# Pair 7's turned probabilities are sent from SP's queue, and the last norm's sums stand one unit later

## The chip, the core and the metric

The program runs on one core of a Trainium2 chip. That core has five engines with a queue of instructions each: TensorE (PE, matmuls; its weight loads are listed apart as PEld), VectorE (DVE), ScalarE (ACT), GpSimd (POOL) and SyncE (SP), which here only issues DMAs. Each engine takes its instructions strictly in the order of the program; they meet through semaphores. A DMA is issued by an instruction in the queue of SP, ACT or POOL and then moved by 16 DMA engines that all queues share. The metric is the device time of one execution in microseconds (us). Before the change it is 640.57 us, the median of 3 runs (640.5 to 640.58).

## What is computed

Two residual layers over 256 tokens of width 1024, float32: layer 0 mixes the tokens with forgetting attention, layer 1 with block attention plus a relative-position bias (with 256 tokens there is one block, so it is causal attention). Behind each mixer come a SwiGLU feed-forward part and a gated embedding, and one norm ends it.

```
for i in range(DEPTH):
    u = _rmsnorm(h, attn_norm_g[i])
    ...
        o = _fox_attention(q, k, v, log_f)
        h = h + _merge_heads(o) @ fox_w_o[j]
    ...
    u = _rmsnorm(h, ffn_norm_g[i])
    gu = u @ ffn_w_in[i]
    h = h + (jax.nn.silu(gu[..., :D_FF]) * gu[..., D_FF:]) @ ffn_w_out[i]
    gate = jax.nn.sigmoid(_rmsnorm(h, ple_norm_g[i]) @ ple_w_gate[i])
    h = h + gate * (p[i] @ ple_w_up[i])
return _rmsnorm(h, final_norm_g)
```

## The kernel before

**Weights.** The float32 weights are streamed in chunks of 128x1024 in the order of use. SP loads a chunk into one of six buffers (`raw`, lines 138, 154 and 186; line 186 loads chunks with a gap in them, 128x1080). ScalarE rounds it to a first half (`whi`, lines 139, 169, 187) and VectorE subtracts to get the rest (`wlo`, lines 142, 171, 188). A product is then three matmuls (lines 94, 95, 96): high by high, high by low, low by high. SP may load into a `raw` buffer again when VectorE has made `wlo` from it, and `whi` and `wlo` have six buffers each, free when TensorE has used them.

**The end of an attention.** The 16 heads go in 8 pairs, 0 to 7. For each pair TensorE makes the scores, VectorE adds the bias or mask (L606), ScalarE makes the exponentials (L610) and scales them (L629). `turn` (lines 632 to 661) then transposes the probabilities on VectorE in blocks of 32 (tile `turn`, L644) and moves the blocks between partitions by DMA into the tile `pt`, from which `values` (lines 667 to 681) multiplies them with `v` into the bank `po` (L674, L676); the result is split into the tile `o` (L319 on ScalarE, L320 on VectorE). Pairs 0 to 4 go through DRAM, pairs 5 to 7 straight from SBUF in four DMAs of 96 KB each (L651). Which queue issues those four is the line

```
queue = nc.scalar if j == NP - 1 else nc.gpsimd
```

so pair 6's stand on POOL and pair 7's on ScalarE. The output projection `wo` has 8 parts (`PARTS`), each with one weight chunk. The order of the end is written out by hand: parts 0, 1 and 2, then `values(4)` (pairs 4 and 5), parts 3 and 4, `values(6)` (pairs 6 and 7), parts 5 and 6, and part 7. ScalarE has, in the same stretch, the scaling of pairs 6 and 7 (L629), two copies into `v` (L513), pair 7's four DMAs (L651) and then the rounding of the weights of part 3 (L139) and of what follows. In layer 0 the chunks of parts 3 and 4 are called whi_1324 and whi_1355, and those of the feed-forward part begin with raw_1519 and raw_1525.

**The last gate.** In layer 1, `ple` (lines 865 to 990) multiplies by the gate's weights in units (`pair_unit`) of two blocks of 128 input channels: four units c = 0 to 3 of 12 matmuls (128x512) for the first half of the output (tile `pg`), then the second half. The norm's factor is applied behind them, by token. `column_root` (lines 277 to 288) makes that factor: `total` adds up the squares on VectorE (L234, L236), two matmuls with a column of ones sum over the channels (bank `pr`, L284), VectorE scales (`ms`, L286), POOL takes the root (`col`, L288). A small activation (L108) loads ScalarE's table for the sigmoid and waits for `col`. `by_token` (lines 894 to 902) turns the residual: four transposes on VectorE (L898) and eight DMAs (L902), two of them on ScalarE's queue and six on SP's. The gates (L913) need `col` and `pg`; the additions (L916) need the turned residual. The second half ends with a narrow bank `pgl`, whose gate, addition, sum of squares (L957), root (L960), scaling (L986, L989) and output DMAs (L964) close the program.

What the scheduler makes of this is a fixed order for each engine; the matmuls L284, called behind unit 1, stood in the middle of unit 2.

Of the kernel before, what the change touches and what calls it, by code (L numbers as in the profile page):

```python
# [38 lines left out]
NP = H // 2  # L39
# [36 lines left out]
def trunk(ctx: ExitStack, tc: tile.TileContext, xg, wx, xr, pt, w, cst, gf, rel, hot, rvm, out):  # L76
    nc = tc.nc
# [28 lines left out]
    def table(func, after=None):  # L106

        nc.scalar.activation(warm, ones if after is None else after, func)  # L108
# [184 lines left out]
    nm = Norm(0)  # L293
# [33 lines left out]
    def pair_unit(bks, c, wt, x, ts=(0, 1), mid=None):  # L327

        for kk in range(2):
            k = 2 * c + kk  # L330
            if kk and mid:
                mid()
            for t in ts:
                tokens(bks[t], x(k), t, [w[:, kk * HC:(kk + 1) * HC] for w in wt], k == 0, k == KT - 1)
# [125 lines left out]
    def attention(layer, nm, mid, early, nf):  # L460
# [84 lines left out]
        def project(j, a):  # L545
# [31 lines left out]
            with tc.issue_after(got.ins):  # L577
                for back in [turn(*x[:2]) for x in far]:
                    back()
# [52 lines left out]
        def turn(j, e):  # L632

            near = j >= DIRECT
            t = work.tile([P, 4, 3, 2, 32], F32, tag="e", bufs=4, name=f"turn{layer}_{j}")  # L640
            for s in range(2):
                src = e[:, s].rearrange("p (b y c) -> p b c y", b=3, c=4) if near else \
                      e[:, s].rearrange("p (b c x) -> p b c x", b=3, x=32)
                nc.vector.transpose(t[:, :, :, s].rearrange("p c b x -> p b c x"), src)  # L644
            p = work.tile([P, 4, 3, 2, 32], F32, tag="pt", bufs=4, name=f"pt{layer}_{j}")
            for s in range(2):
                pts[2 * j + s] = p[:, :, :, s].rearrange("p c b x -> p b c x")
            if near:
                queue = nc.scalar if j == NP - 1 else nc.gpsimd
                for a in range(4):  # L650
                    queue.dma_start(p[:, a].rearrange("p b s x -> p (b s x)"),  # L651
                                    t[32 * a:32 * a + 32].rearrange("p c b s x -> p (c b s x)"))
                return lambda: None
            d = dram.tile([P, 6 * P], F32, name=f"dt{layer}_{j}")
            nc.gpsimd.dma_start(d, t.rearrange("p c b s x -> p (c b s x)"))

            def back():
                for i in range(4):
                    nc.gpsimd.dma_start(p[32 * i:32 * i + 32].rearrange("p c b s x -> p c (b s x)"),
                                        bass.AP(tensor=d.tensor, offset=d.offset + 192 * i,  # L660
                                                ap=[[6 * P, 32], [32 * 6 * P, 4], [1, 192]]))

            return back
# [71 lines left out]
        for x in fresh:  # L735
            scaled(*x)
            turn(*x[:2])
# [127 lines left out]
    def ple(layer, nm, ut, nx):  # L865
# [28 lines left out]
        def by_token(hf):  # L894

            o = end[:, hf].rearrange("p (c t m x) -> p c t m x", c=4, t=2, m=4)
            for t in range(2):
                nc.vector.transpose(o[:, :, t].rearrange("p c m x -> p m c x"),  # L898
                                    h[:, 4 * hf:4 * hf + 4, t * P:(t + 1) * P].rearrange("p m (y c) -> p m c y", c=4))
            for a in range(4):  # L900
                queue = nc.scalar if hf == 0 and a % 2 else nc.sync
                queue.dma_start(ht[:, hf, a].rearrange("p t x -> p (t x)"), end[32 * a:32 * a + 32, hf])  # L902
# [21 lines left out]
        for c in range(4):  # L924
            pair_unit(bks[0], c, half(), nm.k)
            if c == 1:
                with tc.issue_after(nm.column_root().ins):
                    nc.gpsimd.drain()
                table(AF.Sigmoid, nm.col[:, 0:1])
                with tc.issue_after(nm.added.ins):  # L930
                    for hf in range(2):
                        by_token(hf)
        for t in range(2):
            gate(bks[0][t], t, 0, HC)

# [45 lines left out]
        for c0 in (0, HC):  # L981
            c = slice(c0, c0 + HC)
# [9 lines left out]
    for layer in range(2):  # L992
        nf = Norm(3 * layer + 1)
        if layer == 0:
            attention(0, nm, fox_bias, first, nf)
        else:
            attention(1, nm, lambda _: (lambda: moba[2]), [], nf)
        got = []
        np_ = Norm(3 * layer + 2)
        ffn(layer, nf, lambda pp=None: ple_in(layer) if pp is None else got.append(ple_up(layer, pp)), np_)  # L1000
        nm = Norm(3) if layer == 0 else None
        ple(layer, np_, got[0], nm)
# [123 lines left out]
```

## Time and profile before

| what | value |
|---|---|
| median of 3 runs | 640.57 us |
| the profiled execution: its own time | 640.69 us |
| its span, first to last instruction | 638.9 us |
| what lies around the span | 1.79 us |
| TensorE busy | 627.0 us, 98% |
| VectorE, ScalarE, POOL busy | 467.1, 384.6, 42.6 us |
| mean granted TensorE clock | 0.995 |
| weight loads of SP (L154 and L138: 177; L186: 36) | 512 and 540 KB each, 4.4 and 4.5 us to landing |

Start times are us from the start of the span. A row of the timeline gives start, duration, engine, line, operation, output<-input and count; behind it in brackets the idle time of the engine ahead of it and what ended that. "ACTq" and "SPq" are the queues' own instructions, DMAs above all; POOL's DMAs are listed under POOL. A matmul's duration covers the way through the array, so two of 0.28 us can start 0.11 us apart: what counts is the distance between starts. "DMA to landing" runs from the start of the issue to the arrival of the data.

### The profile page before, as it was taken

How to read it: one execution, taken by the hardware profiler on the slowest of the kernel's cores; microseconds unless marked ns; L12 is line 12 of the kernel's file. 1: busy time of each engine (PE TensorE's matmuls, PEld its weight loads, DVE VectorE, ACT ScalarE, POOL GpSimd, SP SyncE). 2: the span in 40 equal slices, each digit the busy share in tenths (PEclk: the TensorE clock that was granted, in tenths of full speed). 3: DMA queues.
4: the chain of work that ended last, by engine and by line, in shares of the span. 5: the costliest groups of instructions: out<-in, count | busy, mean ns of one | idle time of the engine just before them, and what ended most of it. 6: DMA issues, size and time to landing. Idle time of an engine off the chain costs nothing.

```text
span 638.9 us, 13102 instructions
## 1 busy us (share of the span) xinstructions
PE 627.0 (98%) x5241; PEld 604.9 (95%) x5241; DVE 467.1 (73%) x757; ACT 384.6 (60%) x663; POOL 42.6 (7%) x85
## 2 busy tenths in 40 slices
PE   9999989999999999999999999999999999999995
PEld 7899879999999999999989998899999999999984
DVE  7888868886666666668894898788666666666695
ACT  6668866764444445448774798767544444454753
POOL 0103340000000000000000054100000000000001
PEclk9999998999999999999999999999999999999999
DMA  9768878397766566666574697865866666665522
GB/s 341 248 203 242 265 215 287 100 330 259 270 202 199 187 198 214 197 208 177 192 235 171 210 297 216 261 222 170 257 192 194 198 198 199 199 210 180 191 47 86
DMA packets 41885, 135.27 MB, mean 212 GB/s; under 512 B 5248, under 2 KB 10848, under 8 KB 41824
## 3 DMA queue, kind: packets, MB, share of 16 engines
q1 hardware_dynamic: 36464, 123.33, 60.3%
q0 software_dynamic: 3488, 9.44, 5.0%
q10 hardware_dynamic: 1872, 1.67, 0.9%
q8 instruction: 41, 0.67, 0.4%
q14 instruction: 20, 0.16, 0.1%
HBM read 126.01 MB, written 8.15 MB: 210 GB/s over the span
## 4 chain that ended last, share of the span: by engine, by line
PE 82%; DVE 8%; ACT 3%; issue 2%; DMA 2%; SPq 1%; ACTq 1%; POOL 1%; DVEq 0%; POOLq 0%
PE gu L95 13%; PE gu L94 13%; PE gu L96 13%; PE fo L96 6%; PE fo L94 6%; PE fo L95 6%; PE pq L94 3%; PE pq L96 3%; PE pq L95 3%; DVE wlo L171 2%; DVE turn L644 2%; PE v L456 2%; PE wo L94 2%; PE wo L96 2%; PE wo L95 2%
## 5 line engine op out<-in xcount | busy, mean ns | idle before, releaser
L171 DVE TENSOR_TENSOR wlo<-raw,whi 128x1024 fp32r<-128x1024 f32 (+1 forms) x168 | 203.3, 1215 | 65.2 <-ACT whi L169 65.1
L169 ACT ACTIVATE whi<-raw 128x1024 fp32r<-128x1024 f32 x166 | 173.6, 1055 | 95.1 <-issue 42.5
L95 PE MATMUL gu<-g,whi 128*128 128x256 f32 x704 | 194.9, 277 | 0.0
L94 PE MATMUL gu<-g,whi 128*128 128x256 f32 x704 | 194.8, 277 | 0.0
L96 PE MATMUL gu<-g,wlo 128*128 128x256 f32 x704 | 194.7, 277 | 0.0
L96 PEld LDWEIGHTS gu<-g,wlo 128*128 128x128 f32 x704 | 132.3, 188 | 0.0
L95 PEld LDWEIGHTS gu<-g,whi 128*128 128x128 f32 x704 | 132.2, 188 | 0.1
L94 PEld LDWEIGHTS gu<-g,whi 128*128 128x128 f32 x704 | 132.3, 188 | 0.0
L96 PE MATMUL fo<-fp,wlo 128*128 128x256 f32 x352 | 97.4, 277 | 0.0
L95 PE MATMUL fo<-fp,whi 128*128 128x256 f32 x352 | 97.3, 276 | 0.0
L94 PE MATMUL fo<-fp,whi 128*128 128x256 f32 x352 | 97.2, 276 | 0.0
L94 PE MATMUL pq<-g,whi 128*128 128x256 f32 x256 | 71.5, 279 | 0.0
L96 PE MATMUL pq<-g,wlo 128*128 128x256 f32 x256 | 70.9, 277 | 0.1
L95 PE MATMUL pq<-g,whi 128*128 128x256 f32 x256 | 70.8, 277 | 0.0
L188 DVE TENSOR_TENSOR wlo<-raw,whi 128x1080 fp32r<-128x1080 f32 x36 | 45.9, 1281 | 29.8 <-ACT whi L187 29.4
L94 PEld LDWEIGHTS fo<-fp,whi 128*128 128x128 f32 x352 | 66.1, 188 | 0.0
L95 PEld LDWEIGHTS fo<-fp,whi 128*128 128x128 f32 x352 | 66.1, 188 | 0.0
L96 PEld LDWEIGHTS fo<-fp,wlo 128*128 128x128 f32 x352 | 66.1, 188 | 0.0
L187 ACT ACTIVATE whi<-raw 128x1080 fp32r<-128x1080 f32 x36 | 39.6, 1102 | 27.9 <-PE gu L95 27.1
L94 PEld LDWEIGHTS pq<-g,whi 128*128 128x128 f32 x256 | 48.1, 188 | 1.0 <-issue 0.3
L96 PEld LDWEIGHTS pq<-g,wlo 128*128 128x128 f32 x256 | 48.1, 188 | 0.3 <-DVE wlo L171 0.3
L95 PEld LDWEIGHTS pq<-g,whi 128*128 128x128 f32 x256 | 48.1, 188 | 0.1
(194 smaller groups left out, 1043.7 us busy)
## 6 DMA issues: line engine op xcount, KB each, us to landing
raw<-w SPq DMA_DIRECT2D x177, 512.0 KB, 4.4
raw<-w SPq DMA_DIRECT2D x36, 540.0 KB, 4.5
dt<-turn POOLq DMA_DIRECT2D x10, 384.0 KB, 3.4
pt<-dt POOLq DMA_DIRECT2D x40, 96.0 KB, 5.4
d<-d SPq DMA_DIRECT2D x4, 768.0 KB, 7.0
bias<-d SPq DMA_DIRECT2D x4, 512.0 KB, 7.1
pt<-turn POOLq DMA_DIRECT2D x16, 96.0 KB, 4.0
pt<-turn ACTq DMA_DIRECT2D x8, 96.0 KB, 3.7
```

Source lines behind the costliest of these rows:

```text
L94: mm(o, ah, bh, start=start, stop=False, skip_group_check=True)
L95: mm(o, ah, bl, start=False, stop=False, skip_group_check=True)
L96: return mm(o, al, bh, start=False, stop=stop, skip_group_check=True)
L169: state["hi"] = state[f"hi{i}"] = nc.scalar.activation(hi[:, c], raw[:, c], AF.Copy)
L171: nc.vector.tensor_tensor(lo[:, c], raw[:, c], f32(hi[:, c]), op=ALU.subtract)
L187: nc.scalar.activation(ht, raw[:, 0:WW], AF.Copy)
L188: state["lo"] = nc.vector.tensor_tensor(lt, raw[:, 0:WW], f32(ht), op=ALU.subtract)
L456: got = mm(bks[2 * t + hf], x[a][:, t * P:(t + 1) * P], w[b][:, hf * HC:(hf + 1) * HC], start=k + a + b == 0, stop=k + b == KT, skip_group ...
L644: nc.vector.transpose(t[:, :, :, s].rearrange("p c b x -> p b c x"), src)
```

## The change

Two edits. Pair 7's four DMAs in `turn` are issued by SP instead of ScalarE, in both layers. In the last gate `total` and `by_token` stay behind unit 1, while `column_root` (two matmuls, the scaling and POOL's root), POOL's drain and the small activation that loads the table go behind unit 2.

```
@@ -646,7 +646,7 @@
             if near:
-                queue = nc.scalar if j == NP - 1 else nc.gpsimd
+                queue = nc.sync if j == NP - 1 else nc.gpsimd
                 for a in range(4):
                     queue.dma_start(p[:, a].rearrange("p b s x -> p (b s x)"),
                                     t[32 * a:32 * a + 32].rearrange("p c b s x -> p (c b s x)"))
@@ -924,12 +924,14 @@
         for c in range(4):
             pair_unit(bks[0], c, half(), nm.k)
             if c == 1:
+                nm.total()
+                with tc.issue_after(nm.added.ins):
+                    for hf in range(2):
+                        by_token(hf)
+            if c == 2:
                 with tc.issue_after(nm.column_root().ins):
                     nc.gpsimd.drain()
                 table(AF.Sigmoid, nm.col[:, 0:1])
-                with tc.issue_after(nm.added.ins):
-                    for hf in range(2):
-                        by_token(hf)
```

At the end of layer 0's attention, ScalarE's queue loses the four DMAs that stood between the copies into `v` and the rounding of part 3's weights (whi_1324):

```order
 L513 ACTIVATE v<-v_1_165,col_302 128x512
 L513 ACTIVATE v<-v_3_167,col_302 128x512
-L651 DMA pt_7_1217<-turn_7_1214 128x1x192 x4
 L139 ACTIVATE whi_1324<-raw_1323 128x1024
 L169 ACTIVATE whi_1355<-raw_1354 128x1024
```

In the same place SP's queue gets them between the first two weight loads of the feed-forward part:

```order
 L154 DMA raw_1471<-w 128x1024
 L186 DMA raw_1519<-w 128x1080
+L651 DMA pt_7_1217<-turn_7_1214 128x1x192 x4
 L186 DMA raw_1525<-w 128x1080
 L154 DMA raw_1531<-w 128x1024
```

The instructions themselves are the same four; only the queue in which they wait and are issued is another. In layer 1 the same holds, between raw_5454 and raw_5460.

In the last gate TensorE had the two column matmuls in the middle of unit 2, whose chunk is whi_7800:

```order
L96 MATMUL pg_0_1_7733<-whi_7800,g_5450 128x512
L284 MATMUL pr_7778<-first_line,sum_5451 128x1 x2
L94 MATMUL pg_0_0_7732<-whi_7800,g_5450 128x512
L95 MATMUL pg_0_0_7732<-wlo_7801,g_5450 128x512
L96 MATMUL pg_0_0_7732<-whi_7800,g_5450 128x512
L94 MATMUL pg_0_1_7733<-whi_7800,g_5450 128x512
```

Now they stand at its end (the chunk is called whi_7791 in the changed program), six matmuls later, ahead of unit 3:

```order
L94 MATMUL pg_0_1_7733<-whi_7791,g_5450 128x512
L95 MATMUL pg_0_1_7733<-wlo_7792,g_5450 128x512
L96 MATMUL pg_0_1_7733<-whi_7791,g_5450 128x512
L284 MATMUL pr_7808<-first_line,sum_5451 128x1 x2
L94 MATMUL pg_0_0_7732<-whi_7818,g_5450 128x512
```

ScalarE's queue in the same place had the table load and the small activation ahead of its two DMAs of the turned residual:

```order
L169 ACTIVATE whi_7873<-raw_7872 128x1024
L108 ACT_TABLE_LOAD
L108 ACTIVATE first_line<-col_7783 128x1
L902 DMA ut_7585<-end 128x1x256 x2
L913 ACTIVATE pgt_0_0_7835<-pg_0_0_7732,col_7783 128x512
```

and now has them behind:

```order
L169 ACTIVATE whi_7873<-raw_7872 128x1024
L902 DMA ut_7585<-end 128x1x256 x2
L108 ACT_TABLE_LOAD
L108 ACTIVATE first_line<-col_7813 128x1
L913 ACTIVATE pgt_0_0_7835<-pg_0_0_7732,col_7813 128x512
```

The two DMAs went ahead of the table load, which therefore starts when they are issued. On VectorE the scaling L286, which stood behind the first of the four transposes L898, now stands behind the fourth.

More of the change, by code (lines that the diff above doesn't have):

```diff
@@ L648, in turn @@
             if near:
-                queue = nc.scalar if j == NP - 1 else nc.gpsimd
+                queue = nc.sync if j == NP - 1 else nc.gpsimd
                 for a in range(4):
@@ L926, in ple @@
             if c == 1:
+                nm.total()
+                with tc.issue_after(nm.added.ins):
+                    for hf in range(2):
+                        by_token(hf)
+            if c == 2:
                 with tc.issue_after(nm.column_root().ins):
@@ L929, in ple @@
                 table(AF.Sigmoid, nm.col[:, 0:1])
-                with tc.issue_after(nm.added.ins):
-                    for hf in range(2):
-                        by_token(hf)
         for t in range(2):
```

## The prediction

> **What bounds the kernel now.** I read the page first, then the waits of TensorE, then the timeline at the two places where it waits, then the windows over the same stretch for the granted clock.
>
> ```profile
> PE 627.0 (98%) x5241; PEld 604.9 (95%) x5241; DVE 467.1 (73%) x757; ACT 384.6 (60%) x663; POOL 42.6 (7%) x85
> ...
> PEclk9999998999999999999999999999999999999999
> ...
> PE wo L94 <- ACT whi L139: 3.3, 2, 2.1
> ...
> PE pr L284 <- DVE sum L236: 0.3, 1, 0.3
> ```
>
> TensorE is busy for 627.0 of 638.9 us, so this program is as long as TensorE's queue plus its few holes. Between the first matmul and the last gate only two kinds of hole of any size are listed: twice the projection `wo` waits for ScalarE's rounding of a weight chunk (3.3 us together, the longer 2.1), once the column matmuls L284 wait for VectorE's sum. And in one slice alone, the seventh (95.8 to 111.8 us), the clock falls below 9 tenths. The change touches just these places: the first edit the two waits of `wo`, the second that of L284.
>
> **Layer 0, what stands in the way.** The end of the attention; rows of several engines:
>
> ```profile
> 87.09 3.13 DVE L644 STREAM_TRANSPOSE turn<-e 128x384 f32<-128x384 f32 x4
> ...
> 88.58 1.25 ACT L513 ACTIVATE v<-v,col 128x512 f32<-128x512 f32 x2
> ...
> 90.25 3.50 ACTq L651 DMA_DIRECT2D pt<-turn  x4
> ...
> 91.53 0.65 PE L674 MATMUL po<-pt,v 128*64 128x256 f32 x4
> ...
> 94.07 1.06 ACT L139 ACTIVATE whi<-raw 128x1024 fp32r<-128x1024 f32 x1 [4.24 <-DMA pt<-turn]
> ...
> 95.16 1.29 DVE L142 TENSOR_TENSOR wlo<-raw,whi 128x256 fp32r<-128x256 f32 x2 [4.94 <-ACT whi L139]
> ...
> 95.18 0.38 PE L94 MATMUL wo<-o,whi 128*128 128x256 f32 x1 [2.12 <-ACT whi L139]
> ...
> 102.87 0.65 PE L674 MATMUL po<-pt,v 128*64 128x256 f32 x4
> ...
> 104.33 0.39 PE L94 MATMUL wo<-o,whi 128*128 128x256 f32 x1
> ```
>
> ScalarE is through with its arithmetic at 89.83 (88.58 + 1.25). Its next instructions are pair 7's four DMAs, which can't go before the transposes end at 90.22, and whose issue then holds ScalarE's queue until 93.75. Behind them stands the rounding of part 3's weights, 94.07 to 95.13; TensorE starts part 3 at 95.18. Without the four DMAs ScalarE rounds that chunk at once, from 89.9 to 90.95, the next until 92.0, and VectorE, idle from 90.22, has the first `wlo` by about 92.3.
>
> TensorE's `values(4)` starts at 91.53. How long `values` holds TensorE is seen at its next call: from 102.87 to the first `wo` at 104.33, 1.46 us. Part 3 could then start at 92.99, and starts at 95.18: **2.19 us** of hole.
>
> **Layer 0, the slow matmuls behind the hole.** Parts 3 and 4 are 48 matmuls. Their clean pace:
>
> ```profile
> 84.98 0.28 PE L94 MATMUL wo<-o,whi 128*128 128x256 f32 x1
> ...
> 91.10 0.28 PE L94 MATMUL wo<-o,whi 128*128 128x256 f32 x1
> ...
> 102.67 0.28 PE L96 MATMUL wo<-o,wlo 128*128 128x256 f32 x1
> ...
> 104.55 0.28 PE L95 MATMUL wo<-o,whi 128*128 128x256 f32 x1
> ```
>
> From 84.98 to 91.10 stand 54 starts, 0.1133 us each. The first one behind `values` takes 0.22 (104.33 to 104.55), the last ahead of it 0.20 (102.67 to 102.87), so 48 take 0.22 + 46 x 0.1133 + 0.20 = 5.63 us. They took 7.69 (95.18 to 102.87). The windows say why:
>
> ```profile
> 96.00:97.00 1.00, 1.00 (x9) 0.90 (x8) 1.00 (x2) 1.00 (x3) 0.00 (x0) 0.93 0.00 0
> 97.00:98.00 1.00, 1.00 (x7) 1.00 (x6) 1.00 (x2) 1.00 (x2) 0.00 (x0) 0.50 0.76 91
> 98.00:99.00 1.00, 1.00 (x7) 1.00 (x7) 1.00 (x3) 1.00 (x2) 0.00 (x0) 0.50 0.72 281
> 99.00:100.00 1.00, 1.00 (x6) 1.00 (x6) 1.00 (x2) 1.00 (x2) 0.00 (x0) 0.50 0.93 300
> 100.00:101.00 1.00, 1.00 (x10) 1.00 (x9) 1.00 (x2) 1.00 (x2) 0.00 (x0) 0.86 0.94 340
> ```
>
> The column behind POOL's is the granted clock: about 3.4 us at half speed, which cost 0.07 + 3 x 0.50 + 0.14 = 1.7 us. The rest, 0.35, is part 3 waiting piecemeal for `wlo`. I take the dip for a consequence of the hole: it is the only dip and follows the longest hole by under 2 us. Then both go: 7.69 - 5.63 = **2.06 us**. Layer 0 together: 4.25.
>
> On the clock the Trainium skill speaks against me. "TensorE: Matmul & The Clock Gate", section "HAM oscillation — how this bites in real kernels", asks for an idle gap of over 3.4 us before the clock is halved; the gap here has 2.1. The length of the dip agrees with that page's window of 3.4 us, the cause doesn't. By that rule the dip is not this hole's and may stay; that is the first rival below.
>
> **Layer 1.** The same place:
>
> ```profile
> 402.62 2.54 ACTq L651 DMA_DIRECT2D pt<-turn  x4
> ...
> 403.62 0.65 PE L674 MATMUL po<-pt,v 128*64 128x256 f32 x4
> ...
> 406.32 0.38 PE L94 MATMUL wo<-o,whi 128*128 128x256 f32 x1 [1.18 <-ACT whi L139]
> ...
> 412.40 0.65 PE L674 MATMUL po<-pt,v 128*64 128x256 f32 x4
> ...
> 407.00:408.00 1.00, 1.00 (x9) 0.91 (x9) 1.00 (x2) 1.00 (x3) 0.00 (x0) 1.00 0.00 0
> ```
>
> Part 3 could start at 403.62 + 1.46 = 405.08 and starts at 406.32: 1.24 us. Parts 3 and 4 take 6.08 instead of 5.63 at full clock (1.00): 0.45. Layer 1 together: **1.69 us**.
>
> **What is late next.** Pair 7's data must be there when `values(6)` starts: after the change at 92.99 + 5.63 = 98.6 and at 405.08 + 5.63 = 410.7. They now stand in SP's queue:
>
> ```profile
> 87.20 0.33 SPq L186 DMA_DIRECT2D raw<-w  x1
> ...
> 96.53 0.33 SPq L186 DMA_DIRECT2D raw<-w  x1
> ...
> 399.56 8.43 SPq L186 DMA_DIRECT2D raw<-w  x2
> ...
> DMA to landing us min/median/max: 2.2/4.8/7.1
> ...
> raw<-w SPq DMA_DIRECT2D x1, 540.0 KB, 5.0
> ```
>
> SP issues raw_1519 at 87.20 and then nothing until 96.53, when VectorE has freed a buffer; in layer 1 it stands from 399.9 to about 407.7. So SP waits for the transposes where it would wait anyway. The issue on SP isn't in the trace: below, four times a weight load's 0.33 = 1.3 us, above, the 3.50 of ScalarE's queue. I take the latter, the same instructions: free at 93.75 and 405.2. The fourth issue then starts at some 92.3 and 404.5, and with the median landing of all `pt` transfers, 4.8 us, the data are there at 97.1 and 409.3, 1.5 and 1.4 us early; with the longest, 7.1, they are 0.8 and 0.9 us late (an upper end of 1.7 us). Behind them waits raw_1525: its buffer comes free with the first `wlo` at 92.3, so it is held by up to 1.5 us, and still starts 2.8 us earlier than 96.53. VectorE's string of roundings, which TensorE follows, can begin at 91.0 instead of 95.16, 4.2 us earlier, as much as TensorE gains; it then pauses until `values(4)` is out, at 93.0. I cost that at nothing, and at 0.5 us where the string becomes the bound.
>
> The Trainium skill has a rule against the new place: in "DMA: Bandwidth & Descriptors", section "Queues, rings and completion order", a DMA engine takes one queue's descriptors in order and changes between queues by packet. By it, in layer 1 pair 7's data start only when raw_5454 has come, 399.56 + 5.0 = 404.6, about when the fourth is issued anyway; no trace here shows pair 7 on SP's queue. It raises the chance of the second rival, not the sum.
>
> **The last gate.** Column matmuls, and what is beside them:
>
> ```profile
> 614.86 0.39 PE L96 MATMUL pg<-whi,g 128*128 128x512 f32 x1
> 615.50 0.61 PE L284 MATMUL pr<-first_line,sum 128*128 128x1 f32 x4 [0.26 <-DVE sum L236]
> ...
> 616.28 0.39 PE L95 MATMUL pg<-wlo,g 128*128 128x512 f32 x1
> 616.51 0.40 PE L96 MATMUL pg<-whi,g 128*128 128x512 f32 x1
> ...
> 615.05 1.28 ACT L108 ACT_TABLE_LOAD   x1
> ...
> 617.52 2.30 ACTq L902 DMA_DIRECT2D ut<-end  x2
> ...
> 623.25 0.69 DVE L916 TENSOR_TENSOR end<-ut,pgt 128x512 f32<-128x512 f32 x1 [1.31 <-DMA ut<-end]
> ...
> 631.98 0.43 DVE L914 TENSOR_TENSOR pgt<-pgt,ut 128x256 f32<-128x256 f32 x1 [0.72 <-ACT pgt L913]
> ```
>
> At a pace of 0.23 (616.28 to 616.51) TensorE would be free for L284 at 615.09; it starts at 615.50. Six matmuls later, at 615.09 + 6 x 0.23 = 616.5, the sum has long been there: **0.41 us** less. At most the whole visit goes, 616.28 - 614.86 - 2 x 0.23 = 0.96; at least nothing. What the move makes late: the table load comes behind two DMAs that hold ScalarE until 619.82, then 1.28, so the first gates start at some 621.3 instead of 619.93 and are through VectorE by about 623.3. The addition L916 waits for its data until 623.25 anyway; that hides it. VectorE still has 0.72 us to spare ahead of the last gate, of which 0.41 goes.
>
> **Sum.** 4.25 + 1.69 + 0.41 = 6.35 us off 640.69, the profiled execution's own time (638.9 of span and 1.79 around it): 634.34. The median of the runs is 0.12 below that execution, so **634.2 us**. Nothing behind swallows it: TensorE has no other hole in which to lose it, and the weights are loaded as buffers come free, hence relative to TensorE.
>
> **Rivals.**
> 1. The clock dip has another cause and stays. For it: the gap is short, and 1.75 us lie between its end and the dip. Against: no other dip in 638.9 us. It gives back 1.7 us: 635.9.
> 2. A new wait takes the old one's place: pair 7's data come late to `values(6)`. For it: SP's queue has a weight load right ahead of them. Against: the spare time above. Price up to 1.7 us, 635.9.
> 3. ScalarE's rounding finds another wait and the first edit does nothing. Against: the 4.24 us ahead of L139 end with the DMAs' own issue. Only the last gate's 0.41 would remain: 640.2.
> 4. Slower: the same transfers, but so slow behind the weights that `values(6)` starts later than before. That needs a landing of more than 9.4 us ((102.87 - 92.3 + 412.40 - 404.5 + 0.4) / 2); at 10 it would be 641.7. Against: the longest of all is 7.1.
>
> **Chances.** Forecast 0.76 (633.4, with all of L284's visit and 0.2 of a small wait gone, to 635.0); first rival 0.12; second 0.07; third 0.03; fourth 0.02. The range 633.4 to 636.0 takes in the first three of these five. A measurement of this kernel tells about 0.2% (1.3 us) from no change: faster 0.95, same 0.03, slower 0.02.
>
> **What would show it.** In the changed profile the waits of TensorE hold no `wo` for whi L139; the seventh slice of the clock is a 9; from `values(4)` to `values(6)` it is 7.1 us in both layers (11.34 and 8.78 before); L284 stands without an idle time. Wrong would be: half-speed windows near 95 us, a wait of L674 for a DMA, or the second raw load of L186 issued later than 96.5.

## The result, and the profile after

| | kernel before | kernel after |
|---|---|---|
| median of the runs taken together | 640.50 us, 5 runs (640.17 to 640.58) | 634.63 us, 5 runs (634.23 to 635.20) |
| ratio after / before | | 0.9911, 95% interval 0.9896 to 0.9925 |
| the profiled execution, own time and span | 640.69, 638.9 us | 634.63, 632.8 us |
| mean granted TensorE clock of it | 0.995 | 0.997 |

The change makes the kernel 5.9 us (0.9%) faster. The prediction was 634.2, with a range of 633.4 to 636.0. The page of the kernel after, the rows of the engines and of the clock:

```profile
PE 624.2 (99%) x5241; PEld 602.8 (95%) x5241; DVE 467.7 (74%) x757; ACT 384.7 (61%) x663; POOL 43.4 (7%) x85
...
PEclk9999999999999999999999999999999999999998
```

All that its waits of TensorE list (engine, line, what was waited for: us in total, times, longest):

```profile
PE cold L114 <- PEq L1120: 0.8, 1, 0.8
PE v L456 <- ACT g L207: 0.5, 2, 0.3
```

Both waits of `wo` and the one of L284 are gone; the seventh slice of the clock is a 9. What is left waits in the first ten microseconds. TensorE's busy time falls from 627.0 to 624.2: the matmuls at half clock, and those that waited piecemeal for `wlo`, counted as busy.

The end of layer 0's attention in the timeline of the kernel after, ScalarE first, then SP's queue, VectorE and TensorE:

```profile
89.55 1.24 ACT L513 ACTIVATE v<-v,col 128x512 f32<-128x512 f32 x2
90.69 1.06 ACT L139 ACTIVATE whi<-raw 128x1024 fp32r<-128x1024 f32 x1
...
88.16 0.33 SPq L186 DMA_DIRECT2D raw<-w  x1
91.27 3.60 SPq L651 DMA_DIRECT2D pt<-turn  x4
94.99 0.53 SPq L186 DMA_DIRECT2D raw<-w  x1
...
91.78 1.30 DVE L142 TENSOR_TENSOR wlo<-raw,whi 128x256 fp32r<-128x256 f32 x2 [0.57 <-ACT whi L139]
...
92.49 0.65 PE L674 MATMUL po<-pt,v 128*64 128x256 f32 x4
93.94 0.39 PE L94 MATMUL wo<-o,whi 128*128 128x256 f32 x1
99.60 0.65 PE L674 MATMUL po<-pt,v 128*64 128x256 f32 x4
```

ScalarE goes from the copies of `v` straight to the rounding of part 3's weights and is through at 91.75. TensorE is ready for them at 93.94, when `values(4)` is out. From `values(4)` to `values(6)` it is 7.11 us (11.34 before). SP stands in the issue until 94.87 and then loads the next chunk, 1.5 us earlier than the 96.53 of before, though this execution is about 1 us late by then.

The granted clock there (the column behind POOL's):

```profile
97.00:98.00 1.00, 1.00 (x11) 1.00 (x10) 1.00 (x2) 1.00 (x2) 0.00 (x0) 1.00 0.94 336
98.00:99.00 1.00, 1.00 (x11) 1.00 (x11) 1.00 (x2) 0.49 (x1) 0.00 (x0) 1.00 1.02 398
99.00:100.00 1.00, 1.00 (x10) 0.80 (x11) 1.00 (x2) 0.71 (x1) 0.00 (x0) 1.00 1.02 377
```

It is 1.00 where it was 0.50. The same place in layer 1, and the last gate:

```profile
400.30 0.65 PE L674 MATMUL po<-pt,v 128*64 128x256 f32 x4
401.75 0.39 PE L94 MATMUL wo<-o,whi 128*128 128x256 f32 x1
407.42 0.65 PE L674 MATMUL po<-pt,v 128*64 128x256 f32 x4
...
610.94 0.39 PE L96 MATMUL pg<-whi,g 128*128 128x512 f32 x1
611.17 0.50 PE L284 MATMUL pr<-first_line,sum 128*128 128x1 f32 x4
611.53 0.49 PE L94 MATMUL pg<-whi,g 128*128 128x512 f32 x1
611.85 0.40 PE L95 MATMUL pg<-wlo,g 128*128 128x512 f32 x1
```

In layer 1 it is 7.12 us from `values(4)` to `values(6)` (8.78 before). The visit to L284 takes TensorE from 610.94 to 611.85, 0.91 us, where it took 1.42 (614.86 to 616.28).

**Where the time went.** By these distances layer 0 gains 4.23 us, layer 1 1.66 and the visit 0.51. Another 0.3 is gained between layer 1's `values(6)` and the first matmul of the feed-forward part (10.04 and 9.74 us; in `again` it is 10.04 too, so this is no sure gain), and 0.3 behind the last matmul of `pgl`. Together that is 7.0, but the span is only 6.1 shorter. The difference lies ahead of everything that the change touches: TensorE's first matmuls of L377 start 0.6 us later than in the profile of before, and by the first `values` (67.38 and 68.33 us) it is 0.95.

### The profile page after: what moved, and what is told of

It reads as the page before. It is cut to its first block, busy times and chain, and to the rows that moved or that the text cites. A ratio compares the mean times of both kernels' runs of the same rounds, so it can differ in the third digit from the quotient of the medians.

```text
span 632.8 us, 13104 instructions
## 1 busy us (share of the span) xinstructions
PE 624.2 (99%) x5241; PEld 602.8 (95%) x5241; DVE 467.7 (74%) x757; ACT 384.7 (61%) x663; POOL 43.4 (7%) x85
## 4 chain that ended last, share of the span: by engine, by line
PE 92%; DVE 3%; DMA 1%; issue 1%; SPq 1%; ACT 0%; POOL 0%; POOLq 0%; DVEq 0%; ACTq 0%
PE gu L95 13%; PE gu L94 13%; PE gu L96 13%; PE fo L96 6%; PE fo L95 6%; PE fo L94 6%; PE pq L94 5%; PE pq L96 5%; PE pq L95 4%; PE wo L94 2%; PE wo L95 2%; PE wo L96 2%; PE v L94 2%; PE v L95 2%; PE v L96 2%; PE v L456 1%
## 5 line engine op out<-in xcount | busy, mean ns | idle before, releaser
L171 DVE TENSOR_TENSOR wlo<-raw,whi 128x1024 fp32r<-128x1024 f32 (+1 forms) x168 | 203.5, 1216 | 65.1 <-ACT whi L169 64.8
```

Source lines behind the costliest of these rows:

```text
L171: nc.vector.tensor_tensor(lo[:, c], raw[:, c], f32(hi[:, c]), op=ALU.subtract)
```

## The experiments

Each kernel is the kernel after with the edit shown, unless it says otherwise; `before` is the kernel before. Times are medians, with the range. The kernel before ran beside each group and had 640.74, 639.98 and 640.04 us in the three groups.

| kernel | us | `values(4)` to `values(6)`, layer 0 / layer 1 |
|---|---|---|
| before, first profile | 640.69 (that execution) | 11.34 / 8.78 |
| before_twice | 640.46 (639.36 to 641.60, 12 runs) | 10.00 / 8.84 |
| after, first profile | 634.63 | 7.11 / 7.12 |
| again | 634.58 (633.72 to 634.93, 5 runs) | 7.11 / 7.29 |
| e1_sp_only | 634.68 (634.39 to 635.00, 5 runs) | 7.12 / 7.11 |
| e2_norm_only | 640.52 (639.23 to 641.75, 12 runs) | 11.33 / 8.82 |
| e3_pool | 635.17 (634.54 to 635.37, 5 runs) | 7.11 / 7.11 |
| e4_half | 635.58 (634.76 to 636.16, 6 runs) | 7.28 / 7.73 |
| e5_hole2 | 636.17 (636.10 to 637.92, 6 runs) | 7.11 / 9.10 |
| e6_hole4 | 639.20 (638.33 to 640.83, 12 runs) | 7.12 / 12.04 |
| e7_layer0 | 636.07 (635.60 to 637.06, 5 runs) | 7.11 / 8.92 |
| e8_layer1 | 637.50 (636.24 to 638.89, 6 runs) | 9.23 / 7.11 |

### The same kernel again: is the late start the change's?

> The changed kernel, unaltered. In the first profile of it TensorE was already 0.6 us behind the kernel before at its first L377 matmul (16.4 against 15.8 us), ahead of every instruction that the change touches, and 1.0 us behind at 67.4. Theory: that is chance, the first weight load landing late. Then this profile shows another start, 15.6 to 16.6, and the time is 633.8 to 635.0. Rival: the change does it (the same program, but pair 7's DMAs on SP alter something from the start on). Then the first L377 stands at 16.3 to 16.5 again, and the hw load lands 5.7 us after its issue again instead of 4.4.

The first matmuls of L377 by kernel, from the view of that line (durations, then first and last start). In `before`, then in `again`, then in `before_twice`, the kernel before in another execution:

```profile
L377 PE MATMUL pf<-hw,wg x14: 379/380/404, 15.8 to 16.5; 128*32 128x256 f32 x14
```

```profile
L377 PE MATMUL pf<-hw,wg x14: 379/379/403, 16.2 to 16.8; 128*32 128x256 f32 x14
```

```profile
L377 PE MATMUL pf<-hw,wg x14: 379/379/403, 16.6 to 17.3; 128*32 128x256 f32 x14
```

The kernel before itself starts them at 15.8 in one execution and at 16.6 in another; over all profiles of this study they lie between 15.7 and 16.7, with no order by kernel. It is chance, and a difference of two single executions can hold 1 us of it.

### One edit alone

The first edit alone (the last gate's code as before), and the second alone:

```
-                queue = nc.scalar if j == NP - 1 else nc.gpsimd
+                queue = nc.sync if j == NP - 1 else nc.gpsimd
```

> Only the first edit: pair 7's DMAs on SP; the last norm's column passes stand where they stood before. Theory: this edit is worth all but the last gate's 0.5 us, so 634.9 to 635.3; no wait of wo for L139, no window at half clock, 7.1 us from values(4) to values(6) in both layers, and again the wait of L284 for VectorE's sum. Rival: the two edits depend on each other or the second brings more than its 0.5 us; then 636 or more.

```
             if c == 1:
+                nm.total()
...
+            if c == 2:
                 with tc.issue_after(nm.column_root().ins):
```

> Only the second edit: the last norm's column passes one unit later; pair 7's DMAs stay on ScalarE. Theory: worth 0.4 to 0.5 us, 640.0 to 640.2; the wait of 2.1 us of wo for L139, and behind it some 3.4 us at half clock, stand in layer 0 as in the kernel before. Rival (the dip of the clock has another cause than the hole): the hole is there and the half clock isn't, or at another place, and the time is near 638.4.

The first edit alone has 634.68 us, as good as both (634.58) and a little better than the 634.9 to 635.3 that were expected: it is the whole gain that a measurement can tell. The second alone has 640.52 beside 640.74 (ratio 0.9998, 0.9988 to 1.0008), which is no difference; 640.0 to 640.2 were expected. The profiles still show the second edit: the visit to L284 takes 1.43 us in the kernel with the first edit alone and 0.91 in that with the second alone. In the latter the hole stands as before, and behind it the half clock; a row of the timeline of `e2_norm_only`, then two of its windows:

```profile
95.49 0.39 PE L94 MATMUL wo<-o,whi 128*128 128x256 f32 x1 [2.12 <-ACT whi L139]
```

```profile
97.00:98.00 1.00, 1.00 (x6) 1.00 (x7) 1.00 (x2) 1.00 (x2) 0.00 (x0) 0.53 0.37 43
98.00:99.00 1.00, 1.00 (x7) 1.00 (x7) 1.00 (x3) 1.00 (x2) 0.00 (x0) 0.50 0.82 242
```

### Another queue, and half of the DMAs on ScalarE

```
-                queue = nc.sync if j == NP - 1 else nc.gpsimd
+                queue = nc.gpsimd
```

> The changed kernel, but pair 7's four DMAs go on POOL's queue, behind pair 6's four, instead of SP's. Theory: only ScalarE's release counts, and any queue whose engine isn't waited for does as well: 634.2 to 635.0, no wait of wo for L139; POOL issues them at about 92.5 to 95 and they land ahead of values(6) at 99.6. Rival: SP's queue is needed (POOL's issue is slower, or pair 6 stands ahead in its queue): then TensorE waits at values(6) for a DMA, 1 us or more in one of the layers, and the time is 636 or more.

```
-                queue = nc.sync if j == NP - 1 else nc.gpsimd
                 for a in range(4):
+                    queue = (nc.scalar if a < 2 else nc.sync) if j == NP - 1 else nc.gpsimd
```

> The changed kernel, but the first two of pair 7's four DMAs go on ScalarE's queue and the last two on SP's. Theory: only the length of the issue on ScalarE counts. Two of four hold it for some 1.75 us behind the transposes' end instead of 3.5, so L139 is through at about 94.2 where TensorE is ready at 93.9: a hole of 0.2 to 0.4 us in layer 0, none or 0.2 in layer 1, and 634.6 to 635.4 us. Rival: any DMA of pair 7 on ScalarE brings the stall back (its wait for the transposes is what counts, not the issue): then wo waits 1 us or more and the time is 637 or more.

On POOL the gain stays but for some tenths: 635.17, a little above what the theory gave, and no wait of `wo`. What it loses is the rival's wait, in a small form. The timeline of `e3_pool` in layer 1, and its DMA issues between 400 and 402.4 us (name, queue, count, size, median us to landing):

```profile
397.99 4.35 POOL L651 DMA_DIRECT2D pt<-turn  x8 [3.41 <-issue]
...
408.57 0.65 PE L674 MATMUL po<-pt,v 128*64 128x256 f32 x4 [0.71 <-issue]
```

```profile
pt<-turn POOLq DMA_DIRECT2D x5, 96.0 KB, 5.6
```

The eight DMAs follow each other; the last is issued at 401.8, and the longest landing of this stretch is 6.7 us, so 408.5. TensorE, inside `values(6)`, starts pair 7 at 408.57, 0.71 us late. On SP the last issue starts at 401.4 and the longest landing there is 4.4 us. So ScalarE's release is what brings the gain, and SP is the better place by about half a microsecond. The reason is likely that on POOL pair 7's transfers stand behind pair 6's four; no run here separates that from what else moves at that time.

With two of the four on ScalarE, the rows of ScalarE in layer 0 (`e4_half`):

```profile
91.12 1.32 ACTq L651 DMA_DIRECT2D pt<-turn  x2
92.49 1.06 ACT L139 ACTIVATE whi<-raw 128x1024 fp32r<-128x1024 f32 x1 [1.79 <-issue]
```

The rounding stands 1.79 us behind the copies instead of the 4.24 of before, and no wait of `wo` is listed. Parts 3 and 4 still follow VectorE piece by piece: 0.17 us longer in layer 0, 0.61 in layer 1. The time, 635.58, is just above the theory's range and far from the rival's 637: the length of the issue counts, not that a DMA stands there.

### Which layer brings what

```
-                queue = nc.sync if j == NP - 1 else nc.gpsimd
+                queue = (nc.sync if layer == 0 else nc.scalar) if j == NP - 1 else nc.gpsimd
```

> The changed kernel, but pair 7's DMAs are on SP's queue in layer 0 only; in layer 1 they are on ScalarE's as before. Theory: layer 1's hole of 1.2 us and its piecemeal matmuls come back, 1.7 to 2.0 us, 636.3 to 636.7, and a hole of 1.2 us brings no half clock: all runs at 0.996 to 0.998. Rival (every hole can bring the dip, one of 1.2 us too): some runs at 0.995 and 1 us or more longer.

The second kernel has `layer == 1` in that line.

> The changed kernel, but pair 7's DMAs are on SP's queue in layer 1 only; in layer 0 they are on ScalarE's as before. Theory: the hole of 2.1 to 2.2 us of layer 0 and its piecemeal matmuls come back in every run, 2.8 to 3.0 us (637.4 to 637.7), and the dip in about half of the runs, those at 0.994 to 0.995, with 1.3 to 1.7 us more (638.8 to 639.3). Rival (the dip needs both holes, or another place): all at 0.997 and one group.

```profile
403.36 0.39 PE L94 MATMUL wo<-o,whi 128*128 128x256 f32 x1 [1.31 <-ACT whi L139]
```

```profile
94.85 0.39 PE L94 MATMUL wo<-o,whi 128*128 128x256 f32 x1 [1.64 <-ACT whi L139]
```

The first row is of `e7_layer0`, the second of `e8_layer1`. With layer 1 on ScalarE the time is 1.5 us above the kernel after (636.07 against 634.58; 636.3 to 636.7 were expected), the section 1.8 us longer, and all five runs have a clock of 0.996 or 0.997. With layer 0 on ScalarE the six runs fall apart: two at 0.994 and 0.995 with 638.45 and 638.89 us, two at 0.997 with 636.24 and 636.77 (two at 0.996, 636.24 and 638.23). In the profiled execution, one of 636.24, ScalarE's issue took 3.00 us (3.50 in the first profile of before), the hole was only 1.64 us and there was no half clock. So the hole's length differs between executions of the same code. Its section is 2.12 us longer, not the 2.9 that was expected, and it starts 0.3 us earlier than `again`; so the lower group lies below the 637.4 of the theory.

### When does the half clock come?

> The kernel before, unaltered, for the spread of its own runs. In the first group 10 of its 17 runs had a mean granted clock of 0.994 to 0.996 and took 641.06 us on the mean, 7 had 0.997 and took 640.00; a dip of 3.4 us to half clock makes 0.27% of the mean clock. Theory: the hole of 2.1 us in layer 0 is there in every run, the dip behind it only in some, about half. Then a profile of a run at 0.997 shows the hole and no window below 0.9 near 97 us, and the runs fall apart again by 1 us or more with their clock. Rival: the dip belongs to every run and the clocks differ elsewhere; then a profile at 0.997 shows it all the same.

The profile of `before_twice`, timeline and windows at the same place as in the prediction:

```profile
92.38 0.65 PE L674 MATMUL po<-pt,v 128*64 128x256 f32 x4
96.14 0.38 PE L94 MATMUL wo<-o,whi 128*128 128x256 f32 x1 [2.24 <-ACT whi L139]
102.38 0.65 PE L674 MATMUL po<-pt,v 128*64 128x256 f32 x4
```

```profile
97.00:98.00 1.00, 1.00 (x9) 0.91 (x9) 1.00 (x2) 1.00 (x3) 0.00 (x0) 1.00 0.00 0
98.00:99.00 1.00, 1.00 (x11) 1.00 (x11) 1.00 (x2) 1.00 (x2) 0.00 (x0) 1.00 0.74 125
99.00:100.00 1.00, 1.00 (x11) 1.00 (x10) 1.00 (x3) 1.00 (x2) 0.00 (x0) 1.00 0.76 289
```

The same program, the same hole, a little longer even, and no half clock. Of 63 runs of the kernel before in this study 24 had a mean clock of 0.995 or less and took 641.1 us on the mean, 31 had 0.997 or more and took 639.9; 8 lie between, at 0.996. Of the 31 runs of kernels without a hole above 1.3 us (after, `again`, `e1_sp_only`, `e3_pool`, `e4_half`, `e7_layer0`) none is below 0.996. A single run's clock tells the dip only roughly: the profile of `e2_norm_only`, with the dip, has 0.996.

Then a hole put where none stood. In layer 1 ScalarE gets copies of probabilities into tiles that nobody reads, 9 of them and 13:

```
         for x in fresh:
             scaled(*x)
             turn(*x[:2])
+            if layer and x[0] == NP - 1:
+                for i in range(9):
+                    pad = work.tile([P, HC], F32, tag="fp", bufs=4, name=f"pad{i}")
+                    nc.scalar.activation(pad[:, 0:3 * P], x[1][:, 1], AF.Copy)
```

> The changed kernel with 9 activations of 128x384 added on ScalarE in layer 1, between the two copies of v ahead of values(4); they write tiles that nobody reads. They hold ScalarE some 4.1 us and make TensorE wait about 2 us in values(4) or behind it, about as long as the hole of layer 0 was in the kernel before, in a place where no hole of that length stood. Loss without a dip of the clock: 2.1 to 2.7 us, 636.7 to 637.4. Theory (a hole of 2 us brings 3.4 us at half clock in about half of the runs): clocks of 0.995 and of 0.997 both occur among the five runs, the former 1 to 1.7 us longer. Rival, by the Trainium skill's page 'TensorE: Matmul & The Clock Gate', section 'HAM oscillation — how this bites in real kernels' (an idle gap of over 3.4 us is needed): all at 0.997, no window below 0.9.

> As the kernel with 9 added activations, but 13: ScalarE is held some 6 us and TensorE waits about 3.9 us. Loss without a dip 4.0 to 4.7 us, 638.6 to 639.4. Theory: the longer the hole the more runs have the dip; at 3.9 us all or nearly all of the five at 0.995 and 640.2 to 641.1. Rival (the hole's length decides nothing, the dip is layer 0's own): all at 0.997.

The copies were shorter than I had taken them (3.81 us for nine), so the holes are 1.74 and 2.96 us. The longer one with what follows, from the timeline and the windows of `e6_hole4`:

```profile
403.31 0.49 PE L676 MATMUL po<-pt,v 128*64 128x128 f32 x4 [2.96 <-ACT v L513]
```

```profile
403.00:404.00 1.00, 0.69 (x6) 0.52 (x8) 0.00 (x0) 1.00 (x2) 0.00 (x0) 0.78 0.00 0
404.00:405.00 1.00, 1.00 (x8) 0.49 (x4) 0.77 (x2) 1.00 (x2) 0.00 (x0) 0.50 0.00 0
405.00:406.00 1.00, 1.00 (x6) 0.99 (x5) 1.00 (x2) 1.00 (x3) 0.00 (x0) 0.50 0.00 0
406.00:407.00 1.00, 1.00 (x7) 1.00 (x6) 1.00 (x2) 1.00 (x2) 0.00 (x0) 0.51 0.67 86
```

Half clock for 3.4 us (0.22 / 0.50 + 1 + 1 + 0.98), in layer 1, where no profile had it before, and none near 97 us: the dip has moved with the hole. Nine of the 12 runs have 0.995 or less; the two at 0.998 took 638.33 and 638.50, the other ten 638.99 to 640.83. Behind the hole of 1.74 us the profile shows none, and of six runs one, at 0.995, took 637.92 us where the others took 636.1 to 636.5. Runs with a mean clock of 0.995 or less, in order of the hole that the kernel's profile shows: 1.31 us (`e7_layer0`), none of 5; 1.64 us (`e8_layer1`), two of 6; 1.74 us, one of 6; 2.1 to 2.2 us, 24 of 63 of the kernel before and 6 of 12 of `e2_norm_only`; 2.96 us, 9 of 12. The holes of the runs without a profile are not known, so the order is a rough one.

## Why the prediction came out as it did

**Layer 0, hole and slow matmuls (4.25).** Right for the execution from which it was worked out: 11.34 - 7.11 = 4.23. The reason, ScalarE's issue of four DMAs, is shown by the kernels with the DMAs on SP, on POOL and half on each.

**The half clock (1.7 of it).** That it is a consequence of the hole is shown: it goes when the hole goes, and comes with a hole in another place. That it belongs to the hole of every run was wrong. Without it the section takes 10.00 us, 11.34 - 10.00 = 1.34 us less, though its hole is 0.1 us longer; the 48 matmuls alone took 6.24 us (96.14 to 102.38) instead of 7.69, so the dip is worth 1.45 us. And the piecemeal wait for `wlo` is 0.6 (6.24 against 5.63) instead of the 0.35 that I had left for it. Over many runs the change brings about 5.3 us where the kernel before has no dip (639.9 to 634.6) and 6.5 where it has one (641.1 to 634.6). The three runs that the prediction started from lay within 0.08 us of each other and were taken for the kernel's time.

The first rival, that the clock stays low, is out: no profile of a kernel without the hole shows a dip, and none of their runs has a mean clock below 0.996. The third and fourth rivals are out by the time (640.2 and 641.7 against 634.63 measured). On the Trainium skill's page "TensorE: Matmul & The Clock Gate", the section "HAM oscillation — how this bites in real kernels" asks for gaps over about 3.4 us; holes of 2.12 and 2.96 us brought the dip here, so that limit doesn't hold for this kernel. Its section "What's actually happening" has a window of 3413 ns that runs free of the program. Dips of 3.4 us, and a chance that grows with the hole, agree with that. If a dip begins where such a window ends, the window ahead of it held 1.73 us of the hole in the kernel before (the dip begins at 96.86) and all 2.96 us in `e6_hole4`; an estimate from that figure is therefore that some 1.7 us of idle time in one window can be enough, and that a hole of 2.24 us brings no dip when two windows share it. The window itself no run here shows.

**Layer 1 (1.69).** Measured 8.78 - 7.12 = 1.66, and 1.5 in the time of the kernel with this layer put back. No profile shows a half clock behind this layer's hole of 1.2 to 1.3 us.

**Pair 7's data (second rival).** SP's issue took 3.60 and 2.56 us, as on ScalarE. The data were in time on SP, and landed no later than on ScalarE (median 3.6 and 3.2 us, where ScalarE's had 4.2 and 3.3): the weight load ahead of them cost nothing that shows. The last of pair 7's data landed at 96.6 in layer 0 (issued at 94.28, 2.3 us) and 405.8 in layer 1 (401.36, 4.4 us), for `values(6)` at 99.60 and 407.42: 3.0 and 1.7 us to spare, where the prediction gave 1.5 and 1.4. Pair 7's own matmuls come 0.7 us later still. On POOL, behind pair 6's four, the margin of layer 1 was used up.

**The last gate (0.41).** Measured 0.51 us, the same in each profile with this edit; the rest of the visit, 0.91 - 2 x 0.23 = 0.45 us, is its own cost. The cover held: behind the later table load the second of the additions L916 still waited 0.30 us for its data, and VectorE waited 0.86 us for the last gate's activation, so that nothing of the delay reached the end. In the whole time 0.5 us is lost between runs of one kernel that lie 0.6 to 1.2 us apart.

**The sum.** 634.63 measured, 634.2 predicted. By the profiles the three terms gave 4.23 + 1.66 + 0.51 = 6.40 instead of 6.35, and 0.6 came in two places that the prediction had not counted; the late start of this execution took 0.95 back, and that is chance. So the agreement to 0.4 us is better than the method: one execution of each kernel carries up to 1 us of chance at the start and up to 1.5 us of a dip that comes or doesn't.

## What to carry to other kernels

A DMA issue is work in its engine's queue: four of them held ScalarE for 3.5 us, and the weights' rounding behind them was what TensorE waited for. Give late DMAs to a queue that is waiting anyway, and not behind other DMAs that are needed sooner. And a short idle time on TensorE can cost more than itself, but not in every run; read the clock of several executions before its price goes into a sum.

## What the runs showed of the hardware

- Holes of 2.12 and 2.96 us on TensorE were followed by 3.4 us of half clock, and another of 2.24 us, in the same place of the program, was not. The dip doesn't start with the hole's end: it came about 1.7 us behind it in the kernel before, and 0.3 us behind it in `e6_hole4`.
- POOL's root of the last norm (L288) took 0.73 us in the three profiles without the second edit and 1.57 in the nine with it. In the three, VectorE's transposes run beside it; in the nine, VectorE's subtraction L171 does, which starts 0.2 to 0.3 us ahead of the root, and the root ends 0.6 us behind its end in each. In the kernel after:

```profile
614.06 1.21 DVE L171 TENSOR_TENSOR wlo<-raw,whi 128x1024 fp32r<-128x1024 f32 x1
614.30 1.57 POOL L288 TENSOR_TENSOR col<-ms,nhalf 128x2 f32<-128x2 f32 x1 [213.69 <-DVE ms L286]
```

  So the root seems to be held up by the subtraction; no run here has the one without the other, and the cause stays open. ScalarE's small activation L108 waited for the root up to 0.72 us in the nine (1.07 to 1.09 in the three), and that was hidden.
